# Memory-attention scores in two matmuls instead of three, and row maxima turned with a zero-padded stationary, in a hybrid MLA encoder kernel

## The chip, the cores and the metric

The kernel runs on one core of a Trainium2 chip. The metric is the time of one execution in microseconds (us). Three runs of the kernel before gave 1765.35, 1766.88 and 1768.74 us; the median is 1766.88 us.

## The reference

One layer is computed (DEPTH is 1), on a sequence of 2048 tokens of width 1024, with a memory of 256 tokens:

```python
h = rmsnorm(x, norm_g)
proj = h @ w_in          # query latent 384, key/value latent 256, rope key 32, memory query 256, gate 1024
q  = rmsnorm(c_q, q_norm_g) @ w_uq        # 12 heads of 64 + 32 (rope)
kv = rmsnorm(c_kv, kv_norm_g) @ w_ukv     # 12 heads of 64 (key) + 64 (value)
attn    = softmax((q_nope k_nope + q_rope k_rope) / sqrt(96)) v       # 2048 keys
mem_out = softmax(q_mem k_mem / 8) v_mem  # 4 heads of 64, 256 keys, from rmsnorm(mem) @ w_mem_kv
out = rmsnorm(x + (concat(attn, mem_out) * silu(gate)) @ w_out, final_norm_g)
```

Everything is float32 outside; the kernel multiplies in float16 with each operand split into a high and a low half, so that a product is `lo*hi + hi*lo + hi*hi`.

## The kernel before

The work runs in four stages.

**First projection (up to about 245 us).** The 16 token tiles of 128 rows are multiplied with the first 928 columns of `w_in`, in two halves of 24 matmuls each (`gemm1a`). Between the matmuls stand "fill points" (`fill1a`), at each of which one piece of side work is issued: the memory's keys and values (`mem_acc`), and then the memory attention of the tiles before, in five steps per tile (`mem_steps`): `qm` turns the 256 memory queries of a tile and splits them into high and low halves; `mx` multiplies the high halves with the high halves of the keys and takes the row maxima; `fin` turns the maxima from a column into a row, so that they become one more contraction row of the queries (the keys hold the constant -64 in that row); `sc` multiplies the scores and takes the exponentials; `pvs` multiplies with the values. The steps of one tile lie 3 or 4 fill points apart, and steps of neighbouring tiles interleave. In the sums below, "tile 0" is the first tile whose memory attention runs.

**Second projection (245 to 450 us).** The gate columns are multiplied pair of tiles by pair (`gate_pair`), in seven block products of 12 matmuls; the memory attention of the last five tiles and the preparation of the first heads' keys and values fill in.

**Latent attention (450 to 1600 us).** There are 48 groups (12 heads by 4 chunks of 512 queries). A group's maxima are found by 16 matmuls and 16 maximum reductions beforehand (`max_steps`), and its `fin` turns them into a row in the same way as in the memory attention. Then 16 units of scores, exponentials and value products follow.

**Output projection (1600 to 1761 us).**

In the first two stages TensorE's instructions are kept in the order of the program (`strict`); in the latent attention a scheduler decides the order. The order of VectorE, ScalarE and GpSimd instructions comes from the scheduler, but for a few pinned ones. Each engine executes its own list in order.

What the change touches, with lines of the kernel before: `mem_acc` (L502), which allocates the memory keys `kmem` (tile names `V`) and writes their high and low halves out of two PSUM banks (`ps_pv`); `max_steps.fin` (L557); `mem_steps` (L658) with `qm`, `mx`, `fin` and `sc`; and `post_norm` (L421), `post_a0`, `post_a1` and `post_b`, where a scratch tile is moved. The helper `mm` (L115) issues every matmul, so all matmuls have line L116; `evac_hilo` (L135) writes a high half on ScalarE (`acopy`) and the low half, the rest, on VectorE. All vector, scalar and GpSimd instructions have line L91. In the rows, `W` is the pool `W1`, where the turned queries live, `ps_m`, `ps_pv` and `ps_sc` are the PSUM banks by tag, and `V`, `B` and `cn` are pools in SBUF.

In `sc`, each head takes three matmuls for a block of 128 keys; two contract over 64 rows and the third over 65:

```python
mm(o, kt(h, 1, u * P, P), q[0:NOPE, h, 0, :], h == 0, False)
mm(o, kt(h, 0, u * P, P), q[0:NOPE, h, 1, :], False, False)
mm(o, kt(h, 0, u * P, P, 1), q[:, h, 0, :], False, True)
```

In `fin`, one maximum per token is the stationary operand, so it has one column, and the output is one PSUM row at partition 64 or 96:

```python
mm(pr[NOPE:NOPE + 1, h * P:(h + 1) * P], st["mh"][:, h:h + 1], ident16, h == 0, h == MHEADS - 1)
```

Of the kernel before, what the change touches and what calls it, by code (L numbers as in the profile page):

```python
# [17 lines left out]
P = 128  # L18
# [52 lines left out]
def kernel(ctx: ExitStack, tc: tile.TileContext, a, out: bass.AP):  # L71
# [77 lines left out]
    vec.tensor_copy(ident16, ident)  # L149
    ctab = sb.tile([P, NT, 16], F32, name="ctab")  # L150
# [60 lines left out]
    gcol = sb.tile([P, 2 * NK], F32, name="gcol")  # L211
    nc.sync.dma_start(gcol, a["gcols"])
    junk = sb.tile([P, QL], BF16, name="junk")
# [207 lines left out]
    def post_norm(t, p, n, o, g):  # L421
        eng = vec if t < DVE_TO else gps
        st = T("st", [P, 4], F32)
        act.activation(junk[:, 0:n], p, AF.Square, scale=rt[:, t, 0:1], accum_out=st[:, 0:1])
        eng.tensor_scalar(out=st[:, 1:2], in0=st[:, 0:1], scalar1=1.0 / n, scalar2=EPS, op0=ALU.mult, op1=ALU.add)
        rsqrt_on(eng, st[:, 1:2], st[:, 2:3], st[:, 3:4])
        eng.tensor_scalar(out=st[:, 2:3], in0=st[:, 2:3], scalar1=rt[:, t, 0:1], scalar2=None, op0=ALU.mult)
        return lambda: stt(o, p, st[:, 2:3], g, ALU.mult, ALU.mult)

    def post_a0(t, pA):  # L430
        r = rows[t] = T("B", [P, NA + KVL], F32)
        kr = r[:, QL:NA]
        f = post_norm(t, pA[:, 0:QL], QL, r[:, 0:QL], gc[:, 0:QL])
        acopy(kr, pA[:, QL:NA], rt[:, t, 0:1])
        f()
        sm = T("sm", [P, 3, 16], F32)
        rope(kr[:, 0:16], kr[:, 16:32], ctab[:, t, :], stab[:, t, :], sm[:, 0], sm[:, 1], sm[:, 2])

    def post_a1(t, pB):
        f = post_norm(t, pB[:, 0:KVL], KVL, rows[t][:, NA:], gc[:, QL:QL + KVL])  # L440
        acopy(qrow(t), pB[:, KVL:NB], rt[:, t, 0:1])
        f()

    def post_b(t):
        cn = rows.pop(t)
        n = T("B", [P, 10, P], F16)
        for w, o, src in ((3, 0, cn[:, 0:QL]), (2, 6, cn[:, NA:])):
            s3 = src.rearrange("p (j c) -> p j c", j=w)
            acopy(n[:, o:o + w], s3)
            vec.tensor_tensor(n[:, o + w:o + 2 * w], s3, n[:, o:o + w], op=ALU.subtract)  # L450
# [51 lines left out]
    def mem_acc(h, q):  # L502
        if h == 0 and q == 0:
            kmem[0] = T("V", [NOPE + 1, 2, 2, 2, NMEM], F16)
            gps.memset(kmem[0][NOPE:NOPE + 1, :, :, 0, :], -MROW)
            vmem[0] = T("cn", [P, 2, MHEADS, 2 * VD + 1], F16)
            gps.memset(vmem[0][:, :, :, 2 * VD:2 * VD + 1], 1.0 / BS)
# [21 lines left out]
        if q == 1:  # L529
            for i in range(2):  # L530
                if h == 0:
                    for j in range(2):
                        evac_hilo(kmem[0][0:NOPE, i, j, 0, :], kmem[0][0:NOPE, i, j, 1, :],
                                  pp[i][j * 64:(j + 1) * 64, 0:NMEM], IWS)
# [7 lines left out]
    def max_steps(g):  # L542
# [14 lines left out]
        def fin():  # L557
# [5 lines left out]
            mh = T("st", [P, TPC], F16)  # L563
            tsc(mh, mr, 1.0 / MROW, -LN16 / (g.scale * MROW), ALU.mult, ALU.add)
            pr = PT("m")
            for qt in range(TPC):
                mm(pr[g.dim:g.dim + 1, qt * P:(qt + 1) * P], mh[:, qt:qt + 1], ident16, qt == 0, qt == TPC - 1)
            acopy(g.qhi[g.dim:g.dim + 1, :], pr[g.dim:g.dim + 1, :])
# [89 lines left out]
    def mem_steps(t):  # L658
# [3 lines left out]
        def qm():  # L662
            q = st["q"] = T("W1", [NOPE + 1, MHEADS, 2, P], F16)
# [3 lines left out]
            for j in range(2):  # L667
                evac_hilo(q[0:NOPE, j::2, 0, :], q[0:NOPE, j::2, 1, :],
                          pt[j * 64:(j + 1) * 64, 0:2 * P].rearrange("p (i t) -> p i t", i=2))

        def kt(h, hl, o, n, e=0):
            return kmem[0][0:NOPE + e, h // 2, h % 2, hl, o:o + n]

        def mx():
            mc = T("st", [P, MHEADS], F32)
            for i in range(2):
                pm = PT("m")
                for j in range(2):
                    h = 2 * i + j
                    mm(pm[:, j * NMEM:(j + 1) * NMEM], st["q"][0:NOPE, h, 0, :], kt(h, 0, 0, NMEM), j == 0, True)  # L680
                vec.tensor_reduce(mc[:, 2 * i:2 * i + 2], pm.rearrange("p (j k) -> p j k", j=2),
                                        axis=AX.X, op=ALU.max)
            mh = T("st", [P, MHEADS], F16)
            tsc(mh, mc, 1.0 / MROW, -LN16 / (SC_MEM * MROW), ALU.mult, ALU.add)
            st["mh"] = mh

        def fin():
            pr = PT("m")
            for h in range(MHEADS):
                mm(pr[NOPE:NOPE + 1, h * P:(h + 1) * P], st["mh"][:, h:h + 1], ident16, h == 0, h == MHEADS - 1)  # L690
            acopy(st["q"][NOPE:NOPE + 1, :, 0, :], pr[NOPE:NOPE + 1, :].rearrange("p (h t) -> p h t", h=MHEADS))

        def sc():
# [3 lines left out]
            for u in range(2):  # L697
                s = PT(mtag[0])
                for h in range(MHEADS):
                    o = s[:, h * P:(h + 1) * P]  # L700
                    mm(o, kt(h, 1, u * P, P), q[0:NOPE, h, 0, :], h == 0, False)
                    mm(o, kt(h, 0, u * P, P), q[0:NOPE, h, 1, :], False, False)
                    mm(o, kt(h, 0, u * P, P, 1), q[:, h, 0, :], False, True)
# [327 lines left out]
    first = {}  # L1031

    def first_max():
        first["g"] = mla_group(0, 0, 0)
# [440 lines left out]
```

## Time and profile before

| | us |
|---|---|
| runs, median (lowest to highest) | 1766.88 (1765.35 to 1768.74) |
| span of the profiled execution | 1761.3 |
| busy in it: PE (TensorE matmul) | 1677.2 (95%) |
| busy in it: DVE (VectorE) | 1471.3 (84%) |
| busy in it: ACT (ScalarE) | 1279.6 (73%) |
| busy in it: POOL (GpSimd) | 926.3 (53%) |
| mean granted TensorE clock | 0.988 |

The profile shows one execution. Its page gives a span, from the first to the last instruction, and no whole time; the span lies 5.6 us below the median of the runs, which is what lies around it. A matmul's busy time contains its passage through the array, so that matmuls in a stream overlap: what one costs in a stream is the distance from its start to the next start, not its duration. PE reads as busy nearly everywhere for that reason, also where starts lie farther apart than they need to.

### The profile page before, as it was taken

The numbers are of one execution on the slowest core, as the hardware profiler recorded it, in microseconds if no ns is written. First come the engines' busy times: TensorE is split into PE (matmuls) and PEld (weight loads), VectorE is DVE, ScalarE is ACT, GpSimd is POOL, SyncE is SP. The second block draws the span as 40 slices with busy tenths as digits, with TensorE's granted clock in tenths as the row PEclk, the third lists the DMA queues.
The fourth block names the chain that finished last, engine by engine and source line by source line (L and its number), as shares of the span: only waits on it lengthen the run. The fifth ranks groups of instructions, "written<-read, shape, count | busy, mean of one in ns | idle before, by whom it ended". The sixth has DMA issues, their size and how long they took to land.

```text
span 1761.3 us, 38122 instructions
## 1 busy us (share of the span) xinstructions
PE 1677.2 (95%) x14292; PEld 935.8 (53%) x14292; DVE 1471.3 (84%) x2785; ACT 1279.6 (73%) x2642; POOL 926.3 (53%) x1211
## 2 busy tenths in 40 slices
PE   7999999989999999999999999999999999998997
PEld 3554544435455565566555655556556555554443
DVE  6777658777889889998999898988999889987775
ACT  6776657776788778878787777877888778884332
POOL 2766444443355556566665665555344455435553
PEclk9999989999999999999999999999999999999999
DMA  8753350221301012111211132113001134105774
GB/s 291 212 167 111 77 148 25 84 103 49 85 14 25 22 50 72 35 38 23 61 22 38 22 86 34 37 23 95 13 13 37 38 96 97 25 25 124 189 194 141
DMA packets 187034, 133.95 MB, mean 76 GB/s; under 512 B 140193, under 2 KB 162849, under 8 KB 186849
## 3 DMA queue, kind: packets, MB, share of 16 engines
q1 hardware_dynamic: 186560, 130.74, 28.2%
q8 instruction: 111, 1.82, 0.4%
q10 hardware_dynamic: 288, 0.79, 0.1%
q14 instruction: 75, 0.61, 0.1%
HBM read 69.89 MB, written 25.17 MB: 54 GB/s over the span
## 4 chain that ended last, share of the span: by engine, by line
PE 52%; DVE 23%; DMA 8%; ACT 8%; issue 5%; POOL 3%; SPq 0%; DVEq 0%; ACTq 0%; POOLq 0%
PE ps_sc L116 27%; PE ps_pv L116 13%; PE ps_m L116 12%; DVE B L91 11%; DVE st L91 9%; ACT B L91 6%; DMA W<-V 3%; DMA V<-in_x_dram 1%; POOL B L91 1%; DVE V L91 1%; DMA B<-V 1%; DMA W<-B 1%; DVE W L91 1%; DVE sm L91 1%; POOL V L91 1%
## 5 line engine op out<-in xcount | busy, mean ns | idle before, releaser
L116 PEld LDWEIGHTS <-B 128*128 128x128 f16 (+2 forms) x9720 | 638.0, 98 | 504.5 <-issue 47.2
L91 ACT ACTIVATE B<-ps_sc 128x512 f16<-128x512 f32 x1529 | 794.7, 619 | 142.8 <-PE ps_pv L116 84.8
L91 POOL TENSOR_TENSOR B<-B 128x512 f16<-128x512 f32 (+1 forms) x328 | 392.6, 1201 | 495.3 <-ACT B L91 420.1
L116 PE MATMUL ps_sc<-W,B 96*128 96x512 f16 (+1 forms) x2304 | 627.4, 379 | 6.3 <-ACT B L91 3.7
L91 DVE TENSOR_REDUCE st<-ps_m 128x1 f32<-128x512 f32 (+1 forms) x800 | 525.8, 680 | 72.6 <-PE ps_m L116 69.8
L91 DVE TENSOR_TENSOR B<-B 128x512 f16<-128x512 f32 (+1 forms) x494 | 400.7, 819 | 42.1 <-ACT B L91 34.7
L116 PE MATMUL ps_pv<-V,B 128*128 128x129 f16 (+1 forms) x6144 | 384.6, 207 | 16.9 <-DVE B L91 9.7
L116 PEld LDWEIGHTS <-W 128*128 128x128 f16 (+2 forms) x2164 | 205.3, 99 | 236.9 <-issue 38.4
L116 PE MATMUL ps_m<-B,W 96*128 96x512 f16 x768 | 273.6, 381 | 13.7 <-DVE st L91 11.2
L116 PE MATMUL ps_sc<-B,B 128*128 128x512 f16 (+1 forms) x912 | 212.6, 371 | 11.2 <-ACT B L356 6.5
L116 PE MATMUL ps_sc<-B,W 128*128 128x512 f16 x648 | 156.6, 391 | 13.5 <-DVE cn L91 8.3
L91 POOL TENSOR_TENSOR B<-B,B 128x256 f16<-128x256 f32 (+3 forms) x112 | 110.3, 985 | 88.0 <-DVE B L91 80.2
L91 ACT ACTIVATE W<-ps_m 1x512 f16<-1x512 f32 (+2 forms) x144 | 78.1, 542 | 59.9 <-PE ps_m L116 25.0
L91 ACT ACTIVATE B<-B 128x512 f32<-128x512 f32 (+4 forms) x132 | 79.8, 643 | 31.5 <-DVE B L91 15.3
L91 ACT ACTIVATE V<-B 128x256 f16<-128x256 f32 x112 | 40.8, 413 | 75.5 <-DMA W<-V 36.2
L116 PE MATMUL ps_m<-cT,W 128*128 128x512 f16 x360 | 87.7, 383 | 0.0
L116 PE MATMUL ps_sc<-cT,W 128*128 128x512 f16 (+1 forms) x312 | 71.7, 381 | 6.4 <-DVE B L91 6.4
L91 DVE SCALAR_TENSOR_TENSOR B<-sm,st,B 128x64 f32<-128x64 f32 x192 | 73.9, 432 | 0.0
L91 POOL TENSOR_TENSOR st<-st,mhalf 128x1 f32<-128x1 f32 x66 | 42.4, 643 | 58.5 <-DVE st L91 55.9
L116 PE MATMUL ps_m<-W,cT 128*128 128x64 f16 (+1 forms) x1440 | 71.4, 203 | 0.0
L116 PEld LDWEIGHTS <-cT 128*128 128x128 f16 x1440 | 64.5, 98 | 10.9
L91 POOL TENSOR_TENSOR V<-B,V 128x256 f16<-128x256 f32 x70 | 52.5, 768 | 31.9 <-ACT V L91 31.7
(123 smaller groups left out, 1554.0 us busy)
## 6 DMA issues: line engine op xcount, KB each, us to landing
B<-in_xT_dram SPq DMA_DIRECT2D x16, 512.0 KB, 7.3
V<-in_x_dram SPq DMA_DIRECT2D x16, 512.0 KB, 5.3
B<-in_x_dram SPq DMA_DIRECT2D x16, 512.0 KB, 4.7
V<-in_xT_dram SPq DMA_DIRECT2D x14, 512.0 KB, 4.1
wo_scr<-B SPq DMA_DIRECT2D x56, 128.0 KB, 2.0
out_dram<-B SPq DMA_DIRECT2D x14, 512.0 KB, 3.2
spill<-B SPq DMA_DIRECT2D x12, 512.0 KB, 2.8
B<-spill SPq DMA_DIRECT2D x12, 512.0 KB, 3.8
```

Source lines behind the costliest of these rows:

```text
L91: ins = f(*args, **kw)
L116: ins = nc.tensor.matmul(o, lhsT, rhs, start=start, stop=stop, skip_group_check=True)
```

## The change

**Memory scores.** The keys `kmem` get 128 rows. In slot 0 rows 0 to 63 hold the high half and rows 64 to 127 hold it again; in slot 1 rows 0 to 63 hold the low half and row 64 the constant -64. The turned queries `q` get 128 rows too: in slot 0 the high half over the low half, in slot 1 the high half with the maxima in row 64. One matmul over 128 rows then gives `hi*hi + hi*lo`, and a second over 65 rows gives `lo*hi` and subtracts the maximum. `qm` copies the high half to both slots with one ScalarE instruction that is twice as long, and VectorE writes the low half to partitions 64 to 127. `mx` contracts over all 128 rows, and so it reads the low half as well. `mem_acc` has four more ScalarE copies, once, for the second copy of the keys' high half.

**Turning the maxima.** `max_row` puts the four maxima of a token into the last column of a tile `mrow` that is zero elsewhere, and takes 65 columns (memory) or 97 columns (latent attention) as the stationary operand. The output then covers PSUM rows 0 to 64 or 0 to 96, of which the last is used. There is one `mrow` tile, where before a small tile of four rotating buffers was taken each time. In the memory attention the VectorE instruction that scales the maxima (TENSOR_SCALAR `mrow<-st`) moves from the end of `mx` to the beginning of `fin`. GpSimd clears `mrow` at the start, and again before the latent attention.

**Scratch.** The scratch tile `junk`, which ScalarE writes and nobody reads, becomes a part of the row tile of each token tile. Comment lines are removed.

```diff
+    mh = sb.tile([P, 4, QKD + 2], F16, name="mrow")
+    gps.memset(mh, 0.0)
+
+    def max_row(dim, mr, k):
+        tsc(mh[:, :, dim], mr, 1.0 / MROW, k, ALU.mult, ALU.add)
+        pr = PT("m")
+        for n in range(4):
+            mm(pr[0:dim + 1, n * P:(n + 1) * P], mh[:, n, 0:dim + 1], ident16, n == 0, n == 3)
+        return pr[dim:dim + 1, :]
...
-    junk = sb.tile([P, QL], BF16, name="junk")
...
+        junk = rows[t][:, NA + KVL:NA + KVL + QL // 2].bitcast(BF16)
...
-        r = rows[t] = T("B", [P, NA + KVL], F32)
+        r = rows[t] = T("B", [P, DM], F32)
...
-            kmem[0] = T("V", [NOPE + 1, 2, 2, 2, NMEM], F16)
-            gps.memset(kmem[0][NOPE:NOPE + 1, :, :, 0, :], -MROW)
+            kmem[0] = T("V", [P, 2, 2, 2, NMEM], F16)
+            gps.memset(kmem[0][NOPE:NOPE + 1, :, :, 1, :], -MROW)
...
-                        evac_hilo(kmem[0][0:NOPE, i, j, 0, :], kmem[0][0:NOPE, i, j, 1, :],
-                                  pp[i][j * 64:(j + 1) * 64, 0:NMEM], IWS)
+                        km = kmem[0][:, i, j]
+                        src = pp[i][j * 64:(j + 1) * 64, 0:NMEM]
+                        evac_hilo(km[0:NOPE, 0, :], km[0:NOPE, 1, :], src, IWS)
+                        acopy(km[NOPE:P, 0, :], src, IWS)
...
-            mh = T("st", [P, TPC], F16)
-            tsc(mh, mr, 1.0 / MROW, -LN16 / (g.scale * MROW), ALU.mult, ALU.add)
-            pr = PT("m")
-            for qt in range(TPC):
-                mm(pr[g.dim:g.dim + 1, qt * P:(qt + 1) * P], mh[:, qt:qt + 1], ident16, qt == 0, qt == TPC - 1)
-            acopy(g.qhi[g.dim:g.dim + 1, :], pr[g.dim:g.dim + 1, :])
+            acopy(g.qhi[g.dim:g.dim + 1, :], max_row(g.dim, mr, -LN16 / (g.scale * MROW)))
...
-            q = st["q"] = T("W1", [NOPE + 1, MHEADS, 2, P], F16)
+            q = st["q"] = T("W1", [P, MHEADS, 2, P], F16)
...
-                evac_hilo(q[0:NOPE, j::2, 0, :], q[0:NOPE, j::2, 1, :],
-                          pt[j * 64:(j + 1) * 64, 0:2 * P].rearrange("p (i t) -> p i t", i=2))
-
-        def kt(h, hl, o, n, e=0):
-            return kmem[0][0:NOPE + e, h // 2, h % 2, hl, o:o + n]
+                src = pt[j * 64:(j + 1) * 64, 0:2 * P].rearrange("p (i t) -> p i t", i=2)
+                acopy(q[0:NOPE, j::2, :, :], src.unsqueeze(2).to_broadcast([NOPE, 2, 2, P]))
+                vec.tensor_tensor(q[NOPE:P, j::2, 0, :], src, q[0:NOPE, j::2, 0, :], op=ALU.subtract)
+
+        def kt(h, n, o, w):
+            return kmem[0][0:NOPE + 1 if n else P, h // 2, h % 2, n, o:o + w]
...
-                    mm(pm[:, j * NMEM:(j + 1) * NMEM], st["q"][0:NOPE, h, 0, :], kt(h, 0, 0, NMEM), j == 0, True)
+                    mm(pm[:, j * NMEM:(j + 1) * NMEM], st["q"][:, h, 0, :], kt(h, 0, 0, NMEM), j == 0, True)
...
-            mh = T("st", [P, MHEADS], F16)
-            tsc(mh, mc, 1.0 / MROW, -LN16 / (SC_MEM * MROW), ALU.mult, ALU.add)
-            st["mh"] = mh
+            st["mc"] = mc
...
-            pr = PT("m")
-            for h in range(MHEADS):
-                mm(pr[NOPE:NOPE + 1, h * P:(h + 1) * P], st["mh"][:, h:h + 1], ident16, h == 0, h == MHEADS - 1)
-            acopy(st["q"][NOPE:NOPE + 1, :, 0, :], pr[NOPE:NOPE + 1, :].rearrange("p (h t) -> p h t", h=MHEADS))
+            pr = max_row(NOPE, st["mc"], -LN16 / (SC_MEM * MROW))
+            acopy(st["q"][NOPE:NOPE + 1, :, 1, :], pr.rearrange("p (h t) -> p h t", h=MHEADS))
...
-                    mm(o, kt(h, 1, u * P, P), q[0:NOPE, h, 0, :], h == 0, False)
-                    mm(o, kt(h, 0, u * P, P), q[0:NOPE, h, 1, :], False, False)
-                    mm(o, kt(h, 0, u * P, P, 1), q[:, h, 0, :], False, True)
+                    mm(o, kt(h, 0, u * P, P), q[:, h, 0, :], h == 0, False)
+                    mm(o, kt(h, 1, u * P, P), q[0:NOPE + 1, h, 1, :], False, True)
...
     def first_max():
+        gps.memset(mh, 0.0)
```

The scheduler's order moves with it. The first place is ScalarE where the memory keys leave PSUM, just before the memory values are multiplied. `V_921<-ps_pv_925` and `V_921<-ps_pv_926` are the copies of the keys' high half for one half of the heads; `W_149_1205<-B_1145,gcol` scales a gate weight that a DMA has loaded. Before:

```order
L91 ACTIVATE B_1080<-B_811 128x384
L91 ACTIVATE V_921<-ps_pv_925 64x256
L91 ACTIVATE V_921<-ps_pv_926 64x256
L91 ACTIVATE B_1080<-B_811 128x256
L91 ACTIVATE W_149_1205<-B_1145,gcol 128x512
L91 ACTIVATE W_118_839<-B_1057 128x32
```

The same place in the changed kernel, where the names' numbers are a little higher (`V_922` are the keys, `W_149_1210<-B_1150,gcol` is the gate weight):

```order
L91 ACTIVATE B_1085<-B_812 128x384
L91 ACTIVATE V_922<-ps_pv_926 64x256 x2
L91 ACTIVATE V_922<-ps_pv_927 64x256 x2
L91 ACTIVATE B_1085<-B_812 128x256
L91 ACTIVATE W_149_1210<-B_1150,gcol 128x512
L91 ACTIVATE V_922<-ps_pv_926 64x256
L91 ACTIVATE V_922<-ps_pv_927 64x256
L91 ACTIVATE W_118_840<-B_1062 128x32
```

The two last copies out of the PSUM banks now stand behind the gate weight's scaling, where before all copies stood ahead of it.

The second place is VectorE at the maxima of tile 0: two TENSOR_REDUCE find them, and the TENSOR_SCALAR on 128x4 scales them for the turn. Before:

```order
L91 TENSOR_REDUCE st_1235<-ps_m_1236 128x2
L91 TENSOR_REDUCE st_1235<-ps_m_1240 128x2
L91 SCALAR_TENSOR_TENSOR B_1145<-B_1145,gcol,B_1146 128x512
L91 TENSOR_SCALAR st_1244<-st_1235 128x4
L91 SCALAR_TENSOR_TENSOR B_1146<-B_1145,gcol,B_1146 128x512
```

In the changed kernel:

```order
L91 TENSOR_REDUCE st_1240<-ps_m_1241 128x2
L91 SCALAR_TENSOR_TENSOR B_1150<-B_1150,gcol,B_1151 128x512
L91 TENSOR_REDUCE st_1240<-ps_m_1245 128x2
L91 SCALAR_TENSOR_TENSOR B_1151<-B_1150,gcol,B_1151 128x512
L91 TENSOR_SCALAR mrow<-st_1240 128x4
```

The scaling stands behind one more 128x512 instruction than before.

## Rows read from the trace of the kernel before

**Rows 1.** The page: its first line.
```profile
span 1761.3 us, 38122 instructions
```

**Rows 2.** Busy time by stretch: us, each engine's busy time (instructions), clock, DMA share.
```profile
97.00:245.00 148.00, 143.77 (x980) 73.29 (x978) 104.83 (x253) 102.06 (x237) 84.50 (x237) 0.97 0.43 120
245.00:340.00 95.00, 89.59 (x493) 40.78 (x494) 70.51 (x122) 68.01 (x121) 38.19 (x34) 0.91 0.23 73
450.00:1600.00 1150.00, 1110.23 (x11058) 659.09 (x11058) 1032.37 (x1872) 916.63 (x1887) 626.18 (x657) 1.00 0.18 43
```

**Rows 3.** Timeline of PE, memory scores of tile 1: start, us, operation, count.
```profile
121.21 0.38 PE L116 MATMUL ps_sc<-B,B 128*128 128x512 f16 x1
121.52 3.08 PE L116 MATMUL ps_pv<-W,V 64*128 64x128 f16 x24
124.44 0.38 PE L116 MATMUL ps_sc<-B,B 128*128 128x512 f16 x1
```

**Rows 4.** Timeline of PE in the latent attention: streams without a break.
```profile
613.58 2.11 PE L116 MATMUL ps_m<-cT,W 128*128 128x512 f16 x9
615.52 0.81 PE L116 MATMUL ps_sc<-W,B 96*128 96x512 f16 x3
...
626.16 1.50 PE L116 MATMUL ps_m<-W,cT 128*128 128x128 f16 x24
627.50 0.38 PE L116 MATMUL ps_m<-B,W 96*128 96x512 f16 x1
```

**Rows 5.** Timeline of PE: the maxima of tile 0 are turned.
```profile
102.06 1.03 PE L116 MATMUL ps_sc<-B,B 128*128 128x512 f16 x4
103.01 0.38 PE L116 MATMUL ps_m<-ident,st 128*1 128x128 f16 x4
103.33 0.61 PE L116 MATMUL ps_sc<-B,B 128*128 128x512 f16 x2
```

**Rows 6.** Timeline of PE: the maxima of one latent group are turned.
```profile
622.23 0.38 PE L116 MATMUL ps_m<-ident,st 128*1 128x128 f16 x4
622.54 0.39 PE L116 MATMUL ps_m<-B,W 96*128 96x512 f16 x1
```

**Rows 7.** Timeline of PE: two turns of f32 data, and what follows.
```profile
101.41 0.38 PE L122 MATMUL ps_m<-ident,B 128*128 128x128 f32 x2
101.62 1.46 PE L116 MATMUL ps_sc<-B,B 128*128 128x512 f16 x6
```

**Rows 8.** Timeline of ACT and PE where the memory keys leave PSUM.
```profile
84.28 0.65 ACT L91 ACTIVATE V<-ps_pv 64x256 f16<-64x256 f32 x2
86.17 2.81 PE L116 MATMUL ps_pv<-B,B 128*128 128x256 f16 x24 [1.61 <-DVE V L91]
88.02 0.72 ACT L91 ACTIVATE W<-B,gcol 128x512 f16<-128x512 f32 x1 [2.38 <-DMA B<-in_w_in_l_dram]
```

**Rows 9.** Timelines of PE and DVE: the maxima of tiles 0 and 1.
```profile
98.49 0.50 PE L116 MATMUL ps_m<-V,W 64*128 64x256 f16 x3 [0.83 <-ACT W L91]
106.12 0.50 PE L116 MATMUL ps_m<-V,W 64*128 64x256 f16 x3 [1.11 <-ACT W L91]
...
98.90 0.43 DVE L91 TENSOR_TENSOR W<-ps_m,W 64x256 f16<-64x256 f32 x1
101.23 0.16 DVE L91 TENSOR_SCALAR st<-st 128x4 f16<-128x4 f32 x1
107.44 0.43 DVE L91 TENSOR_TENSOR W<-ps_m,W 64x256 f16<-64x256 f32 x1
```

**Rows 10.** Groups of ACT instructions from 90 to 345 us: count, busy us, mean ns.
```profile
L91 ACT ACTIVATE V<-ps_pv 128x512 f16<-128x512 f32 x32 | 19.1, 596 | 15.0 <-PE ps_pv L116 14.9
L91 ACT ACTIVATE W<-ps_m 64x256 f16<-64x256 f32 x32 | 12.1, 377 | 14.7 <-PE ps_m L122 10.8 <-DVE W L91 3.6
```

**Rows 11.** Busy time in a stretch at half clock (columns as in group 2).
```profile
147.28:150.69 3.41, 3.41 (x13) 1.34 (x12) 2.24 (x5) 2.05 (x4) 0.00 (x0) 0.50 0.91 300
```

**Rows 12.** Waits of PE from 460 to 1600 us: in total, times, longest.
```profile
PE ps_m L116 <- DVE st L91: 13.8, 42, 1.2
```

More of the change, by code (lines that the diff above doesn't have):

```diff
@@ L439, in post_a1 @@
     def post_a1(t, pB):
-        f = post_norm(t, pB[:, 0:KVL], KVL, rows[t][:, NA:], gc[:, QL:QL + KVL])
+        f = post_norm(t, pB[:, 0:KVL], KVL, rows[t][:, NA:NA + KVL], gc[:, QL:QL + KVL])
         acopy(qrow(t), pB[:, KVL:NB], rt[:, t, 0:1])
@@ L446, in post_b @@
         n = T("B", [P, 10, P], F16)
-        for w, o, src in ((3, 0, cn[:, 0:QL]), (2, 6, cn[:, NA:])):
+        for w, o, src in ((3, 0, cn[:, 0:QL]), (2, 6, cn[:, NA:NA + KVL])):
             s3 = src.rearrange("p (j c) -> p j c", j=w)
```

## The prediction

> **What bounds the kernel now.** I read the page first [rows 1], then the busy time by stretch [rows 2], and then TensorE's timeline around the instructions that the change touches. The profiled span is 1761.3 us, 5.6 us below the median of the runs, and I take those 5.6 us as unchanged: the sum is made against the span, and its result is subtracted from 1766.9.
>
> The stretches say that PE is the engine to look at. From 97 to 245 us it is busy 143.8 of 148 us while DVE and ACT have 105 and 102 [rows 2]. In the latent attention it has 1110 of 1150 us, with DVE at 1032. But busy is not well used. In a stream the distance from start to start is (615.52 - 613.58) / 9 = 0.216 us for 512 columns and (627.50 - 626.16) / 24 = 0.056 us for 128 columns [rows 4]. The memory scores of a tile are 24 matmuls of 128 columns. The last matmul ahead of them should be over at 121.21 + 0.216 = 121.43, and the next stream starts at 124.44 [rows 3]: 3.01 us, where 24 x 0.056 = 1.34 us would do. The reader is to see that PE waits there for no other engine, and yet stands still between matmuls. The turn of the maxima shows the size of one such stop: the four matmuls ahead of it end their turn at 102.06 + 4 x 0.216 = 102.92, the turn starts at 103.01 and the next stream at 103.33 [rows 5]. That is 0.41 us for four matmuls that need 0.22 us: 0.09 us lost on entering and as much on leaving. In the latent attention the same four take 0.31 us until the next start [rows 6], so 0.09 us on leaving again.
>
> What stops it can be read from the shapes. Stationaries of 96 or 128 rows and 128 columns stream into each other without a stop [rows 4]. A stop stands where a matmul of 64 rows meets one of 65 or 128, or where a stationary of one column meets a wide one. The change removes all of these meetings.
>
> **The change part by part, gains.**
> Scores: 16 matmuls of 128 columns without a stop take 16 x 0.056 = 0.89 us in place of 3.01, so 2.12 us for each of 16 tiles: 33.9 us.
> Maxima of the memory attention: four matmuls over 64 rows become four over 128 rows with the same columns. They enter and leave once; by the stops of the turn that is 0.185 us, 16 times: 3.0 us.
> Turns: 0.41 - 0.22 = 0.185 us, at 16 tiles and 48 latent groups: 11.8 us. This needs a stationary of 65 or 97 columns, which the trace does not have. The nearest rows are a float16 stationary of 128 columns (0.056 us a step [rows 4]) and, farther off, the f32 turns at (101.62 - 101.41) / 2 = 0.105 us [rows 7]. A step shorter than 0.056 has no reason, since the one-column stationary has none. At 0.105 the 256 steps would lose 256 x 0.049 = 12.5 us, more than the whole gain. I take the float16 row, which differs in columns alone, and keep the other end for the range.
> Together 48.7 us of TensorE time.
>
> One rule of the Trainium skill speaks against the wide turn. The trace has the 0.056 us for a full 128 columns only [rows 4]. The page "TensorE: Matmul & The Clock Gate", section "Weight-path perf modes", says that the fast weight load is on when there are 128 weights, and its section on LDWEIGHTS gives columns / 1.2 GHz otherwise. By that, a load of 97 columns takes an estimated 81 ns, longer than its matmul, and the 48 latent turns would give back 48 x 4 x 0.025 = 4.8 us; no row shows such a load.
>
> **Costs.**
> Memory keys: four more ScalarE copies, 0.65 us for two [rows 8]. What counts is where two of them stand: behind the gate weight's scaling, which waited for its DMA until 88.02 and took 0.72 us. The memory values' matmuls need these two banks and started at 86.17, released by VectorE. Now they start at 88.02 + 0.72 + 0.65 = 89.4: 3.2 us later. If the DMA came at once it would be 1.3 us.
> Maxima of the first two tiles: PE already waited there for the high half, until 98.49 and 106.12 [rows 9]. Now it needs the low half too, which VectorE ended at 98.90 + 0.43 and 107.44 + 0.43. With 0.2 us for a longer copy in tile 0, that is 1.0 and 1.8 us: 2.8 us. In the later tiles several us lie in between.
> Longer copies in `qm`: 256 elements from PSUM take 0.377 us, 512 take 0.596 [rows 10]; 0.22 us twice a tile on ACT, beside PE.
> Scaling of the maxima, moved to `fin`: in tile 0 it ended at 101.39 and the turn came at 103.01 [rows 5, 9]. One more VectorE instruction ahead of it still leaves about 0.9 us. I cost it at nothing; with the cover gone it is at most about 0.75 us a tile.
> The moved scratch and the two clears of `mrow`: nothing. ScalarE writes as much as before, and GpSimd, idle for 63 of 148 us [rows 2], does the clears while PE streams. The low half goes to other partitions at the same length; I give that no price either.
>
> **What passes through.** In 97 to 245 us lie the scores, maxima and turns of 11 tiles, 2.49 us each, so 27.4 us, which would make 148 into 120.6. DVE's 104.8 us are then 87% and ACT's 102.1 + 22 x 0.22 = 106.9 us are 89%. In the latent attention DVE is busy for 90% and PE still for 97% [rows 2], so these shares do not forbid it. But both engines run their lists in order, and the distances between `qm`, `mx`, `sc` and `pvs` shrink by 2.3 us or more: I take off 0.5 us a tile, 5.5 us.
> In 245 to 340 us lie five tiles' scores, three maxima and four turns, 11.9 us. There PE is already idle for 5.4 us [rows 2] at a steady pace of gate products, whose banks VectorE and ScalarE must free: half is lost, 6.0 us.
> In the latent attention the turns give 48 x 0.185 = 8.9 us. PE waits for the maxima there in total for 13.8 us [rows 12], and where it waits, the stop on entering was hidden: a third is lost, 3.0 us.
> The clock: the granted clock was 0.50 (1.2 GHz) for 3.41 us right after a score stage [rows 11], the first of three such stretches in the first projection. PE streamed in them, so each cost 1.7 us. The half-empty score stage was what preceded them; with it gone I count half of 5.1, 2.5 us.
> Sum: 48.7 - 3.2 - 2.8 - 5.5 - 6.0 - 3.0 + 2.5 = 30.7 us. Span 1730.6, run 1736.
>
> **Rivals.**
> 1. Everything passes. For it: nothing but PE's own stops shows in most of the first stage. Against it: DVE and ACT near 90%. 48.7 + 5.1 - 3.2 - 2.8 = 47.8 us, so 1719.
> 2. The wide turn is no cheaper: either its loads are not hidden (0.105 a step), or 65 and 97 columns still make the stop. Then 11.8 to 12.5 us are gone from the sum, 1748 to 1749. For it: no row has such a stationary. Against it: 96 rows stream like 128 [rows 4], and columns may do the same. (By the rule of the Trainium skill's page "TensorE: Matmul & The Clock Gate", section "Weight-path perf modes", it would be 1741.)
> 3. ACT and DVE become the bound in the first two stages: a third of the 27.4 us passes, none of the 11.9, 6 us in the latent attention, no clock gain: 9.1 + 6 - 6.0 = 9 us, 1758. For it: their shares after. Against it: they too wait for PE's results, and move up with them.
> 4. Slower: in the latent attention the turn comes up in PE's list before VectorE has scaled the maxima. The scheduler has written that stage's list anew, and in four groups of 48 the turn stands 2 to 21 matmuls earlier. The longest such wait now is 1.2 us [rows 12]. It decides from 30.7 / 48 = 0.64 us more per group on; at 1.2 us in all it would cost 57.6 us and end at 1794. Against it: in the other groups the place is the same or later.
> 5. The stop stays in the scores, if it is not the rows that make it: one matmul in three goes, 128 x 0.056 = 7 us, less the costs of 6.0: 1766.
>
> **How the numbers follow.** Forecast, 1724 to 1746: 0.53. Rival 1: 0.14. Rival 2 beyond that band: 0.12. Rival 3: 0.14. Rival 4: 0.03. Rival 5: 0.04. Differences below 0.2% (3.5 us) can't be told from no change: rival 5 gives about half of its chance to "same" and rival 4 and what I have not thought of go to "slower". That makes faster 0.94, same 0.02, slower 0.04. The time is that of the forecast, 1736 us; the range goes from 1716 (rival 1 with a little more) to 1756 (rival 2 whole, most of rival 3).
>
> **What would show it.** In the profile after: a tile's scores as 16 matmuls with the next stream 0.9 us after their start (not 1.5 or more); the turn with its neighbours at 0.22 us instead of 0.41; the memory values starting 3 us later against the matmuls ahead of them, behind the gate weight; the first projection over near 225 us in place of 245; ACT and DVE busier than 85% there; no stretch at half clock right behind the scores. The prediction is wrong if the distances in the scores stay at 0.09 us and more, if PE shows new waits for VectorE or ScalarE of over 1 us a tile, or if the latent attention, 1150 us now, becomes longer.

## The result, and the profile after

The changed kernel takes 1740.56 us (median of 4 runs, 1739.4 to 1744.33), the kernel before 1767.81 us on the same chip: 27.2 us less, ratio 0.9849 [0.9827, 0.9871]. In a later series it was 1737.46 against 1766.02 us, ratio 0.9839 [0.9814, 0.9865]. The forecast was 1736 us, 30.7 us less.

The span fell less than the median, from 1761.3 [rows 1] to 1739.0 us. The profiled run of the changed kernel took 1740.8 us, 1.8 us more than its span. So most of the 5.6 us between the median and the span before came from profiling an execution that was quicker than the median; it is not time around the span.

The stops are gone. In the changed kernel's timeline of PE (start, us, operation, count) the scores of one tile answer to [rows 3]:

```profile
150.91 0.69 PE L116 MATMUL ps_sc<-B,B 128*128 128x416 f16 x3
151.44 1.09 PE L116 MATMUL ps_pv<-W,V 128*128 128x128 f16 x16
152.37 0.52 PE L116 MATMUL ps_sc<-B,B 128*128 128x416 f16 x2
```

From the scores' first start to the next stream it is now 0.93 us in 13 of the 16 tiles (1.6 to 1.7 in the others), where 24 matmuls took 2.92. The turns in the two stages answer to [rows 5, 6]:

```profile
110.70 0.39 PE L116 MATMUL ps_m<-ident,mrow 128*65 128x128 f16 x4
110.93 0.59 PE L116 MATMUL ps_sc<-B,B 128*128 128x512 f16 x2
...
611.26 0.39 PE L116 MATMUL ps_m<-ident,mrow 128*97 128x128 f16 x4
611.49 0.38 PE L116 MATMUL ps_m<-B,W 96*128 96x512 f16 x1
```

The next start follows after 0.23 us instead of 0.31 or 0.32, and nothing is lost on entering either. A stationary of 65 or 97 columns steps at 0.056 us, like one of 128.

New waits stand in their place. The keys' copies answer to [rows 8], in the changed kernel's timeline:

```profile
86.12 1.56 ACT L91 ACTIVATE V<-ps_pv 64x256 f16<-64x256 f32 x4
90.52 0.72 ACT L91 ACTIVATE W<-B,gcol 128x512 f16<-128x512 f32 x1 [1.61 <-DMA B<-in_w_in_l_dram]
91.27 0.65 ACT L91 ACTIVATE V<-ps_pv 64x256 f16<-64x256 f32 x2
91.69 4.07 PE L116 MATMUL ps_pv<-B,B 128*128 128x256 f16 x24 [6.42 <-ACT V L91]
```

The mechanism is the predicted one, with the last two copies behind the gate weight and its DMA, but the values' matmuls start 5.5 us later, not 3.2, because the DMA landed later too. The granted clock was 0.50 from 87.53 to 94.36 us, so they ran at half clock in part: 24 matmuls in 4.07 us instead of 2.81. And the maxima, which had waited in the first two tiles alone [rows 9], wait in seven of the 13 tiles whose maxima lie in this stage. Here it is in a later tile, on PE and on VectorE:

```profile
134.12 0.27 PE L116 MATMUL ps_m<-V,W 128*128 128x256 f16 x1
136.15 0.50 PE L116 MATMUL ps_m<-V,W 128*128 128x256 f16 x3 [1.76 <-DVE W L91]
...
133.22 2.42 DVE L91 SCALAR_TENSOR_TENSOR W<-B,gcol,W 128x512 f16<-128x512 f32 x2
135.67 0.43 DVE L91 TENSOR_TENSOR W<-ps_m,W 64x256 f16<-64x256 f32 x1
```

The second matmul starts when the low half is written, and VectorE came to it late, behind two gate weights.

The waits of PE from 97 to 238 us in the changed kernel (in total, times, longest), where before it waited for the high halves alone, in two places, 1.9 us in all [rows 9]:

```profile
PE ps_m L116 <- DVE W L91: 10.2, 8, 2.2
PE ps_sc L116 <- DVE W L91: 4.8, 1, 4.8
PE ps_pv L116 <- DVE V L91: 3.0, 5, 2.1
PE ps_pv L116 <- DVE sm L91: 1.1, 2, 0.6
```

The second line is not new: it is the wait ahead of the first gate product, which before took 3.4 us and ended at 246.11 us.

Busy time by stretch, cut at the first maxima, the first gate product and the first and last latent turns; first before, then after (columns as in [rows 2]):

```profile
97.40:246.10 148.70, 143.37 (x978) 73.24 (x977) 105.67 (x254) 102.39 (x238) 85.51 (x239) 0.97 0.44 123
246.10:450.80 204.70, 192.78 (x1072) 90.39 (x1072) 154.75 (x262) 140.08 (x247) 82.00 (x75) 0.95 0.21 67
450.80:1570.10 1119.30, 1083.65 (x10787) 643.34 (x10788) 1009.22 (x1826) 894.41 (x1839) 611.14 (x645) 1.00 0.18 44
```

```profile
104.30:237.90 133.60, 114.45 (x889) 69.09 (x889) 105.22 (x254) 106.19 (x238) 81.92 (x239) 0.99 0.49 139
237.90:438.50 200.60, 180.07 (x1033) 88.88 (x1033) 155.53 (x262) 140.87 (x247) 82.73 (x76) 0.95 0.21 67
438.50:1551.10 1112.60, 1082.20 (x10816) 652.27 (x10816) 1002.27 (x1828) 896.96 (x1845) 616.17 (x646) 0.99 0.17 44
```

The memory stage is 15.1 us shorter, and PE is now idle for 19 us of it where it was idle for 5; DVE has the work of before, ACT 3.8 us more, and both are busy for 79%. The gate stage is 4.1 us shorter, the latent attention 6.7, although in this execution 17.1 us of it ran at a granted clock of 0.50, against 3.4 us before (10.2 us in the changed kernel's second profile). The beginning is 6.9 us longer (97.4 to 104.3 us), and the end 3.3 us shorter, which the changed kernel's second profile does not show (0.4 us).

### The profile page after: what moved, and what is told of

The parts are those of the page before. It is cut to its first block, busy times and chain, and to the rows that moved or that the text cites. A ratio compares the mean times of both kernels' runs of the same rounds, so it can differ in the third digit from the quotient of the medians.

```text
span 1739.0 us, 37840 instructions
## 1 busy us (share of the span) xinstructions
PE 1632.3 (94%) x14164; PEld 938.0 (54%) x14164; DVE 1463.9 (84%) x2785; ACT 1285.3 (74%) x2646; POOL 927.3 (53%) x1213
## 3 DMA queue, kind: packets, MB, share of 16 engines
q1 hardware_dynamic: 186560, 130.74, 27.6%
## 4 chain that ended last, share of the span: by engine, by line
PE 49%; DVE 22%; ACT 10%; DMA 9%; issue 5%; POOL 3%; SPq 0%; DVEq 0%; ACTq 0%; POOLq 0%
PE ps_sc L116 26%; PE ps_m L116 12%; PE ps_pv L116 11%; DVE B L91 10%; DVE st L91 8%; ACT B L91 7%; DMA W<-V 4%; DVE V L91 1%; POOL B L91 1%; DVE W L91 1%; ACT V L91 1%; POOL st L91 1%; ACT W L91 1%; DMA V<-in_w_mem_kv_l_dram 1%; DMA B<-V 1%
## 5 line engine op out<-in xcount | busy, mean ns | idle before, releaser
L91 DVE TENSOR_TENSOR B<-B 128x512 f16<-128x512 f32 (+1 forms) x494 | 389.9, 798 | 74.3 <-ACT B L91 55.2
L116 PEld LDWEIGHTS <-W 128*128 128x128 f16 (+1 forms) x2164 | 208.0, 99 | 247.7 <-issue 40.6
L116 PE MATMUL ps_m<-B,W 96*128 96x512 f16 x768 | 273.4, 383 | 13.0 <-DVE st L91 10.2
L91 POOL TENSOR_TENSOR B<-B,B 128x256 f16<-128x256 f32 (+3 forms) x112 | 113.9, 1017 | 97.1 <-DVE B L91 79.9
L91 ACT ACTIVATE W<-ps_m 64x512 f16<-64x512 f32 (+1 forms) x144 | 85.0, 590 | 40.8 <-PE ps_m L116 15.2
L91 ACT ACTIVATE B<-B 128x512 f32<-128x512 f32 (+5 forms) x132 | 79.9, 642 | 33.3 <-DVE B L91 15.8
L91 POOL TENSOR_TENSOR st<-st,mhalf 128x1 f32<-128x1 f32 x66 | 38.2, 579 | 54.7 <-DVE st L91 52.6
```

Of the source, the lines that this page charges most:

```text
L91: ins = f(*args, **kw)
L116: ins = nc.tensor.matmul(o, lhsT, rhs, start=start, stop=stop, skip_group_check=True)
```

## The experiments

Starts are us from the span's start, read from the timelines; "memory stage" goes from the first maxima to the first gate product, "latent" from the first to the last latent turn; "half clock" is the time at a granted clock of 0.50 in the memory stage.

| kernel | ratio to before [95%] | first maxima | memory stage | latent | half clock |
|---|---|---|---|---|---|
| before | 1 | 97.4 | 148.7 | 1119.3 | 10.2 |
| changed | 0.9849 [0.9827, 0.9871] | 104.3 | 133.6 | 1112.6 | 3.6 |
| changed again (c1) | 0.9839 [0.9814, 0.9865] | 103.9 | 133.3 | 1109.0 | 3.4 |
| e13 turn alone | 0.9943 [0.9925, 0.9961] | 97.1 | 155.9 | 1110.7 | 27.6 |
| e14 scores alone | 0.9911 [0.9893, 0.9930] | 103.4 | 133.1 | 1121.2 | 4.9 |
| e9 scratch alone | 1.0053 [1.0035, 1.0070] | 103.7 | 151.9 | 1117.9 | 17.2 |
| e4 turn and scratch | 0.9951 [0.9926, 0.9977] | 103.2 | 155.7 | 1110.7 | 28.0 |
| e6 third matmul | 0.9847 [0.9828, 0.9866] | 105.1 | 136.9 | 1107.3 | 5.3 |
| e1 maxima from high halves | 0.9826 [0.9800, 0.9851] | 104.4 | 131.6 | 1105.9 | 4.7 |
| e2 maxima with a zero row | 0.9839 [0.9814, 0.9864] | 103.8 | 133.2 | 1107.9 | 4.8 |
| e3 keys on GpSimd | 0.9813 [0.9784, 0.9842] | 100.3 | 134.8 | 1106.9 | 6.9 |
| e11 keys on GpSimd, maxima later | 0.9812 [0.9786, 0.9839] | 101.1 | 139.4 | 1107.2 | 18.6 |
| e12 keys on GpSimd, other scratch | 0.9814 [0.9796, 0.9831] | 100.0 | 135.7 | 1107.3 | 5.5 |
| e7 turn of 128 columns | 0.9866 [0.9848, 0.9883] | 105.1 | 133.3 | 1115.0 | 5.5 |

**The parts alone.** The scratch first needed a place that moves little. The row tile of the token tile before is still in use, so that the sum of squares waits for no new tile. No run has this scratch alone; in e13, which has it, the first maxima start at 97.1 us, as before (97.4).

```diff
-        junk = rows[t][:, NA + KVL:NA + KVL + QL // 2].bitcast(BF16)
+        junk = rows.get(t - 1, rows[t])[:, NA + KVL:NA + KVL + QL // 2].bitcast(BF16)
```

e13 has this scratch and `max_row`, with the scores of before:

> The kernel before with the wide turn alone, and the scratch in the row tile before, where it moves nothing. The prediction's terms for the turn are 11.8 us less 3.0 lost in the latent attention: 8.8 us, ratio 0.995. Rival (what the kernel with turn and scratch, 5.9 us faster than before, and the scratch alone, 8.9 us slower, say together): 14.8 us, ratio 0.9915. The latent attention alone should be 5 to 7 us shorter.

Measured: 10.0 us faster (1756.61 against 1766.64 us), by the interval 7 to 13. The latent attention was 8.6 us shorter. The memory stage, though, was 7.2 us longer, and its granted clock shows why. The stretch in e13:

```profile
97.10:253.00 155.90, 149.47 (x979) 78.74 (x978) 105.55 (x254) 102.54 (x238) 82.21 (x240) 0.91 0.41 117
```

The clock is 0.91, before 0.97. There are eight stretches of 3.41 us at half clock right behind the tiles' scores, which still have their stops, where before there were three [rows 11]. At nearly twice the time for each matmul (a turn steps at 107 ns there, else at 56), 17.4 us more at half clock are about 8.7 us, more than the 7.2 us. So the 10.0 us are what is left of a larger gain.

e14 has the same scratch and the scores' part, with the one-column turn of before:

> The kernel before with the scores' part of the change alone (two matmuls, keys and queries of 128 rows, maxima over 128 rows), the turn with one column as before, and the scratch in the row tile before. The prediction's terms: 33.9 + 3.0 gained, less 3.2 (keys), 2.8 (first maxima), 5.5 and 6.0 not passed on, plus 2.5 of clock: about 23 us, ratio 0.987. Theory after the result (the maxima's waits for the low half cost more than was foreseen): 18 to 22 us, ratio 0.9875 to 0.990. Rival (additive with the scratch at 9 us and the turn at 9 us): 27 us, ratio 0.9845.

Measured: 16.2 us by the medians (1750.41 against 1766.64), 15.7 by the ratio: less than all three. The memory stage is as short as in the changed kernel and the first maxima as late. So alone the scores' part gives about 16 us and the turn about 10. That this sums to nearly the whole change (27 to 29 us) does not show that the parts add: e13 contains a loss by the clock that the changed kernel does not have.

e9 has the scratch of the change alone:

> The kernel before with one edit: the scratch tile is a part of each token tile's row tile. The prediction put this at nothing. In the changed kernel the first maxima start 6.9 us later than before, and in the kernel with the turn alone 5.8 us later, though that one has no second copies of the keys; three waits for VectorE between 44 and 82 us, 0.4 to 1.7 us each, are new in both. Theory (the scratch edit does it: ScalarE's sum of squares now writes a row tile that VectorE and the DMA must have left, so it waits earlier): the first maxima start 4 to 6 us later than before here too, and the kernel is 2 to 6 us slower than before, ratio 1.001 to 1.004. Rival (the turn's zero tile or the scheduler's order does it): the first maxima within 1.5 us of before, ratio 0.999 to 1.001.

Measured: 8.9 us slower, the theory's direction, but beyond its 2 to 6 us. The timeline of ACT before has the sum of squares of one tile at 65.79 us, ahead of a memory weight that comes by DMA:

```profile
65.79 0.58 ACT L91 ACTIVATE junk<-ps_sc,rt 128x384 bf16<-128x384 f32 x1 [0.41 <-PE ps_sc L116]
...
73.07 1.33 ACT L91 ACTIVATE B<-V,gcol 128x512 f16<-128x512 f32 x2 [1.86 <-DMA V<-in_w_mem_kv_l_dram]
```

With the scratch in the tile's own row tile the scheduler puts it behind that weight, in e9:

```profile
74.56 1.33 ACT L91 ACTIVATE B<-V,gcol 128x512 f16<-128x512 f32 x2 [1.04 <-DMA V<-in_w_mem_kv_l_dram]
75.80 0.56 ACT L91 ACTIVATE B<-ps_sc,rt 128x384 bf16<-128x384 f32 x1
```

What hangs on it comes later, and the first maxima start 6.3 us later. Not all of the 8.9 us need come from there: the memory stage is 3.2 us longer with 17.2 us at half clock (10.2 before), and the granted clock of e9's four runs is 0.981 to 0.983, against 0.984 to 0.987 in the runs of the kernel before beside them. No run separates the two. e4, the turn with the scratch of the change, mixes both edits:

> The kernel before with the wide zero-padded turn alone (and the moved scratch); the scores stay at three matmuls per head and keys of 64 and 65 rows. Theory (0.185 us a turn, two thirds of it passing in the latent attention): 5 to 9 us faster than the kernel before, ratio 0.995 to 0.997; the latent attention shorter by about 6 us, the memory stage by about 2. Rival (the 18.95 - 12.35 = 6.6 us that the latent attention gained come from the scheduler's new order, not from the turn): the four turns' distance shrinks to 0.22 us and the time moves by less than 3 us.

Measured: 5.9 us faster by the medians, but its runs reach from 1747.37 to 1763.89 us, farther than any other's. The granted clock goes with it: three runs at 0.987 and 0.988 took 1747 to 1749 us, seven at 0.978 to 0.983 took 1758 to 1764. The profile is of one of the seven, with 28.0 us of the memory stage at half clock; its latent attention is 8.6 us shorter than before, its memory stage 7.0 us longer. So the same program differs by some 11 us with the clock, and e13's four runs stand at 0.981 to 0.983 too.

**Number or stops.** e6 adds a third whole-array matmul to each product of the scores, with a tile of zeros:

```diff
                     mm(o, kt(h, 0, u * P, P), q[:, h, 0, :], h == 0, False)
+                    mm(o, kt(h, 0, u * P, P), zero, False, False)
```

> The changed kernel with a third matmul per head and block in the scores, over the whole array, that adds a product with zeros: as many matmuls as before the change, but none over 64 rows. Theory (the stops between 64-row and whole-array matmuls made the scores slow, not their number): the scores of a tile take 24 x 0.056 = 1.34 us to the next stream, 0.45 us more than in the changed kernel and 1.67 us less than before; at most 7 us slower than the changed kernel, ratio to the kernel before 0.985 to 0.989. Rival (the number of matmuls, or their waits for loads, counts): 2.5 us or more per tile, and the ratio is near 0.997.

Measured: 1739.93 us, 2.5 us above the changed kernel of the same series. The scores of one tile in e6:

```profile
142.55 0.22 PE L116 MATMUL ps_pv<-W,V 128*128 128x128 f16 x1
142.61 0.22 PE L116 MATMUL ps_pv<-zero,V 128*128 128x128 f16 x1
142.66 0.28 PE L116 MATMUL ps_pv<-W,V 65*128 65x128 f16 x2
...
143.87 0.22 PE L116 MATMUL ps_pv<-W,V 65*128 65x128 f16 x1
143.93 1.46 PE L116 MATMUL ps_sc<-B,B 128*128 128x512 f16 x6
```

24 matmuls take 1.38 us, against 2.92 before for as many. So the stops were what cost, as the theory says. The 2.5 us by the medians are within the noise of the two. The memory stage shows more; first the changed kernel in its second profile, then e6:

```profile
103.90:237.20 133.30, 114.62 (x890) 69.19 (x891) 106.15 (x254) 106.18 (x238) 81.68 (x239) 0.99 0.48 139
105.10:242.00 136.90, 119.35 (x977) 74.38 (x977) 108.56 (x254) 106.92 (x238) 79.54 (x240) 0.98 0.49 134
```

The stage has 87 matmuls more, 87 x 0.056 = 4.9 us of TensorE work, and is 3.6 us longer (3.3 against the first profile), up to 1 us of it by the clock. So added TensorE work still lengthens this stage: the waits have not taken the pace from TensorE altogether.

**The maxima's waits.** e1 finds the maxima from the high halves alone, as before the change:

```diff
-mm(pm[:, j * NMEM:(j + 1) * NMEM], st["q"][:, h, 0, :], kt(h, 0, 0, NMEM), j == 0, True)
+mm(pm[:, j * NMEM:(j + 1) * NMEM], st["q"][0:NOPE, h, 0, :], kt(h, 0, 0, NMEM)[0:NOPE], j == 0, True)
```

> The changed kernel, but the maxima are found from the high halves alone over 64 rows, as before the change. In the changed kernel's trace the four matmuls of the maxima lose 16.0 us in nine waits that end with VectorE's subtraction of the low half (longest 4.4 us). Theory (they wait because they now read the low half): the waits go, the stop on entering and leaving comes back at 16 x 0.19 = 3.0 us; net gain over the changed kernel 6 to 13 us, so a ratio to the kernel before of 0.977 to 0.981. Rival (they wait because ScalarE's copies are twice as long, or because TensorE now simply runs ahead of both engines): the waits stay, ended by ScalarE or a little further on, and the time is that of the changed kernel plus up to 3 us, a ratio of 0.985 to 0.987.

e2 takes the second slot over 65 rows, with row 64 cleared, so that no low half is read and no stop returns:

```diff
+            gps.memset(q[NOPE:NOPE + 1, :, 1, :], 0.0)
...
-mm(pm[:, j * NMEM:(j + 1) * NMEM], st["q"][:, h, 0, :], kt(h, 0, 0, NMEM), j == 0, True)
+mm(pm[:, j * NMEM:(j + 1) * NMEM], st["q"][0:NOPE + 1, h, 1, :], kt(h, 0, 0, NMEM)[0:NOPE + 1], j == 0, True)
```

> The changed kernel, but the maxima are found from the second slot of the queries (high half in rows 0 to 63) over 65 rows, where row 64 is cleared by GpSimd for each tile: no low half is read, and the matmul is still one of the whole array. Theory (low half): the waits of 16.0 us go and no stop comes back: 8 to 16 us faster than the changed kernel, 2 to 4 us faster than with 64 rows; ratio 0.975 to 0.980. Rival (longer copies): 0.984 to 0.986, with the waits ended by ScalarE. If the clearing on GpSimd comes late, the waits show GpSimd as releaser.

Measured: 0.9826 and 0.9839, while the changed kernel has 0.9849 and 0.9839: neither reaches what the theory asked for, and e2 gains nothing that can be told. (The expectations' 16.0 us in nine waits take in the second projection; PE's list of waits has 14.5 us there, 10.2 of it in the memory stage.) The five largest waits of PE in e2 from 97 to 238 us:

```profile
PE ps_sc L116 <- DVE W L91: 5.4, 1, 5.4
PE ps_pv L116 <- DVE sm L91: 4.6, 4, 2.1
PE ps_pv L116 <- DVE V L91: 3.5, 5, 1.0
PE ps_m L116 <- ACT W L91: 1.6, 3, 0.7
PE ps_m L116 <- DVE W L91: 1.5, 1, 1.5
```

The maxima wait for 3.1 us instead of 10.2, and the scores and values (`ps_pv`) for 8.1 instead of 4.1; the stage is as long as it was (133.2 us). In e1, whose list adds up to 14.6 us where the changed kernel's has 19.1, it is about 2 us shorter (131.6). So the low half was what ended the wait, but most of the stage's length does not hang on it.

e11 gives the maxima five more fill points, with the GpSimd copy of e3:

```diff
-    MEM_OFF = (0, 3, 7, 11, 14)
+    MEM_OFF = (0, 8, 12, 16, 19)
```

> The changed kernel with the keys' second copy on GpSimd and with the maxima five fill points later (offsets 0, 8, 12, 16, 19 in place of 0, 3, 7, 11, 14), all else as it is. Theory of distance (the maxima wait because the chain of two copies and two subtractions does not fit into three fill points that have become shorter): the waits of the maxima, 16.0 us in the changed kernel, go, and no others take their place; 8 to 14 us faster than with the GpSimd copy alone, ratio 0.973 to 0.977. Rival theory (ScalarE and VectorE in order are the bound of the memory stage, so that a wait taken away comes back at another place, as with the maxima from the high halves): the maxima wait less and the scores or values more, ratio 0.979 to 0.983.

Measured: 0.9812, no better than e3's 0.9813: the rival's number. The waits move on, as in e2: the maxima wait for 5.9 us instead of e3's 9.9, the scores and values for 6.3 instead of 3.7, and one turn for 4.4. But the memory stage also ran at half clock for 18.6 us, against 6.9 in e3, and so the trial of distance is not a clean one. That ScalarE and VectorE, each in the order of its list, set the pace of the stage fits e2 and e11; it is not shown, and e6 speaks against it as the whole account.

**The keys.** e3 takes the second copy off ScalarE and out of PSUM:

```diff
-                        acopy(km[NOPE:P, 0, :], src, IWS)
+                        gps.tensor_copy(km[NOPE:P, 0, :], km[0:NOPE, 0, :])
```

> The changed kernel, but the second copy of the memory keys' high half is made by GpSimd from SBUF instead of by ScalarE from PSUM, so that the two banks come free with the first copies. In the changed kernel the memory values' matmuls start 5.5 us later than before (91.69 against 86.17 us), wait 6.4 us for ScalarE, and then run at half clock. Theory (the banks are held by the two copies that stand behind the gate weight): they start near 87 us again, the wait is 1 to 2 us, and 4 to 7 us of the time come back, part of it perhaps lost in later waits: ratio 0.981 to 0.983. Rival (the stretch is bound by the gate weight's DMA or by the keys themselves): the start moves by less than 2 us, ratio 0.984 to 0.986.

Measured: 0.9813, about 6 us better than the changed kernel in its first series and 4.5 in its second, though the intervals overlap. The values' matmuls in e3 start where the theory has them:

```profile
87.25 4.44 PE L116 MATMUL ps_pv<-B,B 128*128 128x256 f16 x24 [2.52 <-DVE V L91]
89.88 0.72 ACT L91 ACTIVATE W<-B,gcol 128x512 f16<-128x512 f32 x1 [3.75 <-DMA B<-in_w_in_l_dram]
```

They no longer stand behind the gate weight. Up to the first gate product e3 is ahead by 2.1 to 2.8 us (235.1 us against 237.2 and 237.9); the rest lies behind it, above all in the latent attention, where the changed kernel's two profiles have more time at half clock (17.1 and 10.2 us, e3 3.4). e12 adds the scratch of e13 and e14:

> The changed kernel with two edits: the keys' second copy on GpSimd, and the scratch laid into the row tile of the token tile before, which is still in use then, so that the sum of squares waits for no new tile (with this scratch alone the orders of ScalarE, VectorE and GpSimd are those of the kernel before). Theory (the scratch edit cost 9 us, as alone, and the copies 4 to 6): 8 to 14 us faster than the changed kernel, ratio 0.975 to 0.980, and the first maxima start at 96 to 99 us. Rival (the scratch's 9 us and the copies' wait are the same wait, which GpSimd's copy has removed already): the ratio of the GpSimd copy alone, 0.981.

Measured: 0.9814, the rival. The scratch costs 8.9 us in the kernel before and nothing that can be told beside the rest of the change. So its price is not one of the edit by itself; that it belonged to one order of ScalarE's list is likely and not shown. e3, e11 and e12 are the fastest versions here, 1733 us each; only the whole of e12's interval lies below the changed kernel's 0.9839.

**The load of 97 columns.** e7 makes the turn's stationary 128 columns wide:

```diff
-            mm(pr[0:dim + 1, n * P:(n + 1) * P], mh[:, n, 0:dim + 1], ident16, n == 0, n == 3)
+            mm(pr[:, n * P:(n + 1) * P], mh[:, n, :], ident16, n == 0, n == 3)
```

> The changed kernel with a stationary of all 128 columns in the turn (31 or 63 more zero columns behind the maxima). The Trainium skill's page 'TensorE: Matmul & The Clock Gate', section 'Weight-path perf modes', has the fast weight load on for 128 weights only. The changed kernel's 97-column turns step at 0.056 us when nothing is waited for, and 0.04 us longer in all where the turn waited for VectorE. If the load of 97 columns is the slower one, 128 columns take these 0.04 us away where the turn waits (13 groups: 0.5 us in all, not to be seen in the time); in a stream nothing changes. Ratio that of the changed kernel, 0.983 to 0.986. Rival (the load binds in a stream too): 5 us faster.

Measured: 0.9866, not faster; its interval overlaps the changed kernel's. From the first to the fourth start a turn in a stream takes 168 ns in both kernels. Where it had waited for VectorE it takes 207 ns with 97 columns and 178 with 128. The difference lies in the first step alone (95 ns against 67); the steps behind it take 56 ns. So a load of 97 columns is slower by some 30 ns where nothing hides it, which is paid once per wait, and behind a running matmul it is hidden. That a load of fewer than 128 columns is the slower one agrees with the Trainium skill's page "TensorE: Matmul & The Clock Gate", section "Weight-path perf modes", which has the fast weight load on for 128 weights. The 81 ns a step that the prediction estimated from that page are not seen in a stream.

c1 is the changed kernel once more:

> The changed kernel itself once more, as the measure for the others of this series: a ratio to the kernel before of 0.983 to 0.987.

Measured: 0.9839.

## Why the prediction was right

**The stops: right.** Three matmuls over 64 and 65 rows became two without a stop, and the turn lost its stop on both sides. The term of 33.9 us for the scores was 16 x (2.92 - 0.93) = 31.8 us on TensorE, and e6 shows that it was the stops.

**The turn: right in mechanism, and near in size partly by luck.** The forecast was 8.8 us, e13 gave 10.0. The wide stationary took no time (rival 2 falls). But the 10.0 us are made up otherwise than the forecast: the latent attention 8.6 us shorter, where 5.9 were forecast; the second projection 3.8 us shorter, where half of four turns, 0.4 us, was forecast; and the memory stage 7.2 us longer, with half clock behind the scores, which I had not thought of.

**What passes in the memory stage: mis-sized.** The 2.8 us for the first two tiles came true: their maxima wait 4.6 us instead of 1.9. The steps "I take off 0.5 us a tile" and "In the later tiles several us lie in between" failed. Five later tiles wait 5.6 us for the low half, the scores and values 4.1 us, and the wait ahead of the first gate product grew by 1.4. With the 2.7 us of the first two tiles that is 13.8 us of new waits, all ended by VectorE, where I had 8.3 (2.8 and 5.5). Over the stage's 11 tiles it is 1.25 us a tile, more than the 1 us that the prediction itself named as a sign that it is wrong. The stage got 15.1 us shorter where the same terms say 21.6 (27.4 - 2.8 - 5.5 + 2.5); e14 gave 16 us for the scores' part instead of 23. Two more of the signs did not come: the stage ended at 237.9 us, not near 225, and ACT and DVE are busy for 79% there, not 85%. e2 and e11 show that a wait taken away at one place comes back, in part, at the next. That points to rival 3, the two engines in the order of their lists, but only in part, as e6 shows. The comparison with the latent attention, where DVE is busy for 90% and PE still for 97%, did not carry over.

**The keys: right in mechanism, too small.** 3.2 us forecast, 5.5 us measured in the start; the gate weight, whose DMA is waited for, came 2.5 us later (90.52 against 88.02 us).

**The scratch: the step "nothing" was wrong for the edit alone,** 8.9 us by e9, part of it perhaps clock; in the change its price is not seen (e12). I had looked at the instruction's length and not at the tile it now has to wait for.

**The clock: right behind the scores, missed elsewhere.** No stretch at half clock stands behind the scores of the memory stage any more. Its 10.2 us became 3.6, of which 3.4 lie among the waits of tile 1's maxima (114.84 to 118.25 us); half of the difference, 3.3 us, compares with the forecast's 2.5. At the keys' wait 6.8 us came up, but PE stood still in most of them, and the values' matmuls lost 1.3 us. What the forecast did not have is the latent attention, with 17.1 us and 10.2 us at half clock in the two profiles against 3.4.

**The total.** By the stages of the two profiles the forecast gave about 8 us too much: 6.5 in the memory stage, 3.7 in the beginning and 1.8 in the second projection, less 0.8 in the latent attention and 3.3 at the end. By the medians it gave 3.5 us too much, or 2.1 in the later series. The two counts differ because the profile before is of an execution quicker than its median and at a higher clock (0.988 against 0.984). I took the whole 5.6 us as lying around the span, where 1.8 do; that alone brought the forecast time 3.8 us nearer to the measured one. So to come within 4.6 us was partly luck.

What stays open is what sets the pace of the memory stage now, and which instruction of the two lists ends the chain there; no run took the longer copies of `qm` away by themselves.

## What to carry to other kernels

Read the distance from start to start, not busy time: a TensorE that reads 97% busy had stops of 0.09 us where matmuls over 64 rows, or with one stationary column, met others, and rows or zero columns that fill the shape removed them, with steps still at 0.056 us. When one engine is to give back a fifth of a stage, do not credit all of it: here about half arrived, with the next engines busy for 79%, and a wait that was removed came back in part elsewhere. Price an edit by the tile that it now waits for: a scratch write of unchanged length, alone, made the kernel up to 9 us slower. And look at the granted clock of each stage before two times are compared.

## What the runs showed of the hardware that was not expected

With the turn's stops gone and the scores' stops left (e13), the granted clock was at 1.2 GHz for 27.6 us of the memory stage, against 10.2 before and 3.6 with both gone. In e11, with both gone as well but with the maxima issued later, it was 18.6 us. So an edit that shortens one part can cost clock beside another; what exactly the clock answers to was not tried.
